# Seven more of the 21-matmul products in the two feed-forward parts of a decoder layer, and accumulating transfers among the down products

## The chip, the cores and the metric

The kernel runs on one core of a Trainium2 chip. The time is the device time of one execution in microseconds (us); the figure for a kernel is the median of several executions. The core has five engines with instruction streams of their own, each in a fixed order: TensorE (PE in the profile, its weight loads PEld), VectorE (DVE), ScalarE (ACT), GpSimd (POOL) and SyncE (SP). The streams meet only at semaphores. SP issues nearly all loads; POOL issues the accumulating transfers spoken of below.

## The reference

One decoder layer on 256 tokens of width 2048, all in float32: a feed-forward half, two token mixers side by side, a second feed-forward half, and a gated embedding, with a layer norm behind each. The part that is changed is the feed-forward half, which occurs twice (f1 and f2):

```
def swiglu(x, w_gu, w_down):
    g, u = jnp.split(x @ w_gu, 2, axis=-1)
    return (jax.nn.silu(g) * u) @ w_down

h = layer_norm(alpha * h + 0.5 * swiglu(h, w_ffn1_gu[i], w_ffn1_down[i]), ...)
... mixers ...
h = layer_norm(alpha * h + 0.5 * swiglu(h, w_ffn2_gu[i], w_ffn2_down[i]), ...)
```

`w_gu` is 2048 x 11264 and `w_down` 5632 x 2048. All weights (484 MB are read in one execution) pass through the core once.

## The kernel before

**Numbers.** Each float32 operand is split into a high and a low part of a shorter matmul type: ACT casts the high part (`hf_gu`, `hf_down`, line 124), DVE subtracts it from the original for the low part (`lf_gu`, `lf_down`, line 128). A product is three matmuls of 128 x 512: low by high, high by high, high by low (lines 418 to 420).

**Chunks and units.** Weights come in chunks of 128 x 1024 float32 (512 KB, one load on SP's queue). A unit of work takes two chunks: the same 256 rows of the sum for two groups of 512 columns. (In the names `lf2_gu_8_0_3` the parts are: f2, gate and up, block 8, chunk 0 of the unit, pair 3.) There are three kinds:

- P, a plain pair: 24 matmuls; two casts on ACT, two low parts on DVE.
- T, a plain pair whose second low part is made otherwise: ACT multiplies the chunk by -1 into the low part's tile (line 133), where it stands rounded, as minus the high part, and POOL's queue issues a transfer of 512 KB that adds the chunk itself to it (`transfer()`). It spares DVE a subtraction.
- S, a "seven": the four block products of a 2 x 2 split are formed by seven products, as in Strassen's and Winograd's scheme, so 21 matmuls. It needs sums of weight blocks, which DVE makes (lines 208 to 217): five operations on 128 x 512 and three on 128 x 1024, in the order u, u, v, `lf`, v, the low part of b, `luf`, `lvf`; ACT casts `hf`, `b`, `huf` and `hvf` for it. It also needs sums of blocks of the activations ("forms", lines 492 to 495, then a split), one group for two neighbouring pairs. The seven's own products collect in banks named `f28s`, `f1d0s` and so on, which are evicted at the end of a block (lines 526 to 530). The last seven of a block takes its low parts in an earlier order, so that 13 of its matmuls stand behind the last of them.

**Stages.** In each feed-forward half, gate and up are made in 11 blocks of 512 columns (j = 0 to 10), with 8 units each; then the down product in two halves of 1024 columns (d0 and d1, in the profile `f1d` and `f1e`), with 22 units each over the 5632 rows. Sevens stand in all gate and up blocks but the first, and in both down halves. Between units hang other pieces of work: in the down halves `before_unit(u)` converts the activations to high and low (`convert`, lines 99 and 100), makes the forms of groups 6 to 9, in f1 runs the rotary table in small pieces on DVE (lines 868 to 893), and at the start come the evictions of the last gate and up block (lines 526 to 530 and 1026 to 1028).

**What sets the order.** A list of all units in order (`plan`) is made beforehand. `fill()` issues loads ahead along this list as far as slots of the weight memory are free (`others(n)` sets how many), and `make_next()` makes a unit's parts some units ahead. So the order of the instructions on each engine is fixed when the program is built. `gu_units` gives the units of a gate and up block (sevens on pairs 0 to 3, order `PTSSPSST`), `down_units` those of the down halves.

Of the kernel before, what the change touches and what calls it, by code (L numbers as in the profile page):

```python
# [16 lines left out]
P = 128  # L17
S = 256
# [9 lines left out]
KF = FF // P  # L28
# [9 lines left out]
HELD_PAIRS = 2, 3  # L38
# [2 lines left out]

SEVEN = (0, 1, 2, 3)

AHEAD = {1: (4, 5), 2: (4,), 3: (4, 5), 4: (4,), 5: (4, 5), 7: (4, 5)}
AHEAD_SLOTS = 32

SEVEN_DOWN = (6, 7, 8, 9)

BIG = 3.0e38
MAGIC = 12582912.0  # L50
# [6 lines left out]
def layer(ctx: ExitStack, tc: tile.TileContext, io):  # L57
# [16 lines left out]
    def slot(shape, dt, name):  # L74
        return slots.tile(shape, dt, tag="slot", name=name)
# [22 lines left out]
    def split(dst_hi, dst_lo, src, lo_engine=None):  # L98
        act.copy(dst_hi, src)  # L99
        (lo_engine or dve).tensor_tensor(dst_lo, src, dst_hi, ALU.subtract)  # L100
# [243 lines left out]
    def slots_for_weights(n, ahead=45, far=90):  # L344
        room.update(slots=n, ahead=ahead, far=far)
# [139 lines left out]
    def seven_forms(full, hi, lo):  # L485


        a11, a21 = (full[:, 0::2, t * P : (t + 1) * P] for t in range(2))
        a12, a22 = (full[:, 1::2, t * P : (t + 1) * P] for t in range(2))
        raw = slot([P, 8, P], F32, "sums")  # L490
        f5, f6, f7, f3 = (raw[:, 2 * j : 2 * j + 2, :] for j in range(4))
        dve.tensor_tensor(f5, a21, a22, ALU.subtract)
        dve.tensor_tensor(f7, a11, a21, ALU.subtract)
        dve.tensor_tensor(f6, f5, a11, ALU.subtract)
        dve.tensor_tensor(f3, a12, f6, ALU.add)
        split(hi, lo, raw)
        return lambda e: [(hi[:, 2 * j + e, :], lo[:, 2 * j + e, :]) for j in range(4)]
# [401 lines left out]
    def gu_units(name, j):  # L899
        if j == 0:  # L900
            return [("P", p) for p in range(KD // 2)]
        if name == "f2" and j in AHEAD:
            return units_of(*(("PPSDSDSP", SEVEN[:3]) if j % 2 else ("PPSSDSSP", SEVEN)), AHEAD[j])
        return units_of("PTSSPSST", SEVEN)

    def gu_keys(name, j):
        return lambda n, p: (name + "_gu", j, n, p)

    def down_units(n_held):


        first = [("P", p) for p in range(2 * SEVEN_DOWN[0])]
        g = SEVEN_DOWN[0]
        sevens = [2 * h for h in SEVEN_DOWN[:3]] + [2 * SEVEN_DOWN[2] + 1, 2 * SEVEN_DOWN[3]]
        plain = [p for p in range(2 * g, KF // 2) if p not in sevens]
        plain = [p for p in plain if p < 2 * SEVEN_DOWN[2]] + sorted(
            (p for p in plain if p >= 2 * SEVEN_DOWN[2]), key=lambda p: p < 2 * SEVEN_DOWN[3] + 2
        )
        while sevens or plain:
            for kind, of in (("S", sevens), ("P", plain)):  # L920
                if of:
                    first.append((kind, of.pop(0)))
        plain = [p for p in range(KF // 2) if p // 2 not in SEVEN_DOWN]
        second = [("P", p) for p in plain[:2]]
        rest = plain[2:]
        for g in SEVEN_DOWN:
            for e in range(2):
                second += [("S", 2 * g + e), ("P", rest.pop(0))]
        return first, second + [("P", p) for p in rest[:-n_held]], rest[-n_held:]

    def down_keys(name, b):
        return lambda n, p: (name + "_down", 2 * b + n, p)

    def plan_ffn(name):
        for j in range(KF // 4):
            block_units(gu_units(name, j), gu_keys(name, j))
        first, second, held = down_units(HELD_PAIRS[name == "f2"])
        block_units(first, down_keys(name, 0))
        block_units(second, down_keys(name, 1))
        plan.extend(Single(down_keys(name, 1)(n, p)) for n in range(2) for p in held)  # L940

    def ffn(name, i, ht, norm, keep, residual, keepers, away):
# [3 lines left out]
        raws = []  # L946
        made = {}
# [27 lines left out]
        def convert(g):  # L975
            hi, lo = (slot([P, 4, S], F32R, f"{name}a{w}{g}") for w in "hl")
            split(hi, lo, raws[g])
            acts[g] = hi, lo

        for j in range(KF // 4):  # L980
# [20 lines left out]
            def before(u, j=j, offset=KD // 2 - len(units)):  # L1001
# [7 lines left out]
                if j == 0 and u == 7:  # L1009
# [12 lines left out]
            if got:  # L1022
                g, v = got
# [5 lines left out]
            else:  # L1029
                v = slot([P, 2, 512], F32, f"{name}v{j}")  # L1030
# [12 lines left out]
        y = {}  # L1043
        space = big.tile([P, 2 * len(SEVEN_DOWN), 8, P], F32R, tag="ht", name=name + "forms")
        made = {}
        first, second, held = down_units(HELD_PAIRS[name == "f2"])
# [12 lines left out]
        def before_unit(u):  # L1059
            if u == 0 and name == "f1":  # L1060
                lazy.append(rotary_table("r"))
            g = u // 2 + 2
            others(2 * KF // 4 - max(0, KF // 4 - 1 - g) + (2 if u >= 10 else 0))
            if u % 2 == 0:
                if 2 <= u < 2 + 2 * len(SEVEN_DOWN):
                    at = u // 2 - 1
                    made[SEVEN_DOWN[at]] = seven_forms(raws[SEVEN_DOWN[at]], space[:, 2 * at], space[:, 2 * at + 1])
                if g < KF // 4:
                    convert(g)
            if u in (11, 12):  # L1070
                y[u - 11] = load_columns(residual, u - 11, name + "y")

# [98 lines left out]
    def mixers(ht, norm, residual, keepers, away):  # L1171
# [691 lines left out]
```

## Time and profile before

| what | value |
|---|---|
| median of 3 runs | 2256.92 us (2256.03 to 2258.23) |
| the profiled execution | 2261.72 us |
| its span | 2259.6 us |
| granted clock of PE, mean | 0.998 |
| PE busy | 2243.5 us (99%) |
| DVE busy | 1995.2 us (88%) |
| ACT busy | 1345.4 us (60%) |
| accumulating transfers of gate and up | 28, 8.0 us each from issue to landing |
| f1's first down half (PE) | 459.70 to 577.30 us |
| f2's blocks 8 to 10 (second seven of block 8 to their end) | 1814.10 to 1926.15 us |
| f2's first down half | 1926.15 to 2042.43 us |

Times in the profile are of one execution, counted from the start of its span; a row gives start, duration, engine, line, operation, what it writes and reads, and in brackets the time that the engine stood before it and what released it. Rows of one line and kind that follow each other are drawn together (x2, x3). Windows give each engine's busy time in a stretch. A PE at 99% is a PE that is nearly always occupied, so what is worth knowing is in which stretches another engine is as full as it is.

### The profile page before, as it was taken

The numbers are of one execution on the slowest core, as the hardware profiler recorded it, in microseconds if no ns is written. First come the engines' busy times: TensorE is split into PE (matmuls) and PEld (weight loads), VectorE is DVE, ScalarE is ACT, GpSimd is POOL, SyncE is SP. The second block draws the span as 40 slices with busy tenths as digits, with TensorE's granted clock in tenths as the row PEclk, the third lists the DMA queues.
The fourth block names the chain that finished last, engine by engine and source line by source line (L and its number), as shares of the span: only waits on it lengthen the run. The fifth ranks groups of instructions, "written<-read, shape, count | busy, mean of one in ns | idle before, by whom it ended". The sixth has DMA issues, their size and how long they took to land.

```text
span 2259.6 us, 28888 instructions
## 1 busy us (share of the span) xinstructions
PE 2243.5 (99%) x10291; PEld 1856.3 (82%) x10291; DVE 1995.2 (88%) x2636; ACT 1345.4 (60%) x1586; POOL 26.7 (1%) x37
## 2 busy tenths in 40 slices
PE   9999999999999999999999999999999999999998
PEld 7888888888888788888788888788888887888887
DVE  6999999989988999889779788689998899889877
ACT  6776776766554554535556554466666677655543
POOL 0000000000000000000000000000000000000000
PEclk9999999999999999999999999999999999999999
DMA  9787887775676779866447568787979978656772
GB/s 312 227 259 240 231 262 225 217 248 188 214 290 255 260 254 312 277 231 207 138 143 247 172 221 288 268 288 248 304 260 272 309 227 245 221 187 219 290 265 73
DMA packets 260920, 541.92 MB, mean 240 GB/s; under 512 B 62620, under 2 KB 67100, under 8 KB 260776
## 3 DMA queue, kind: packets, MB, share of 16 engines
q1 hardware_dynamic: 254760, 522.82, 68.7%
q0 software_dynamic: 4032, 14.68, 3.5%
q10 hardware_dynamic: 1984, 2.58, 0.3%
q8 instruction: 81, 1.33, 0.2%
q14 instruction: 63, 0.52, 0.1%
HBM read 484.43 MB, written 29.36 MB: 227 GB/s over the span
## 4 chain that ended last, share of the span: by engine, by line
PE 89%; DVE 5%; DMA 3%; issue 1%; ACT 1%; SPq 0%; ACTq 0%; DVEq 0%
DMA rf_gu<-in_f_gu 3%; PE rqk L369 3%; PE f1g L420 2%; PE f1g L419 2%; PE f1g L418 2%; PE f1u L419 2%; PE f1u L418 2%; PE f1u L420 2%; PE f2g L419 2%; PE f2g L418 2%; PE f2g L420 2%; PE f2u L419 2%; PE f2u L418 2%; PE f2u L420 2%; PE aqk L369 2%; PE f2d L418 2%
## 5 line engine op out<-in xcount | busy, mean ns | idle before, releaser
L128 DVE TENSOR_TENSOR lf_gu<-rf_gu,hf_gu 128x1024 fp32r<-128x1024 f32 x236 | 281.6, 1218 | 16.0 <-ACT hf_gu L124 15.0
L124 ACT CAST hf_gu<-rf_gu 128x1024 fp32r<-128x1024 f32 x264 | 271.2, 1047 | 40.7 <-DMA rf_gu<-in_f_gu 37.5
L124 ACT CAST hf_down<-rf_down 128x1024 fp32r<-128x1024 f32 x150 | 153.1, 1050 | 66.8 <-DMA rf_down<-in_f_down 51.9
L128 DVE TENSOR_TENSOR lf_down<-rf_down,hf_down 128x1024 fp32r<-128x1024 f32 x150 | 178.0, 1219 | 14.2 <-ACT hf_down L124 6.5
L128 DVE TENSOR_TENSOR lw_in_f<-rw_in_f,hw_in_f 128x1024 fp32r<-128x1024 f32 x140 | 166.4, 1217 | 3.1 <-ACT hw_in_f L124 3.1
L124 ACT CAST hw_in_f<-rw_in_f 128x1024 fp32r<-128x1024 f32 x140 | 142.0, 1051 | 33.2 <-DMA rw_in_f<-in_w_in_f 24.9
L214 ACT CAST hvf_gu<-vf_gu 128x1024 fp32r<-128x1024 f32 x76 | 80.1, 1054 | 84.6 <-DVE vf_gu L213 73.3
L211 ACT CAST huf_gu<-uf_gu 128x1024 fp32r<-128x1024 f32 x76 | 80.1, 1054 | 55.3 <-DVE uf_gu L209 52.8
L216 DVE TENSOR_TENSOR luf_gu<-uf_gu,huf_gu 128x1024 fp32r<-128x1024 f32 x76 | 92.6, 1218 | 1.1 <-ACT huf_gu L211 0.8
L217 DVE TENSOR_TENSOR lvf_gu<-vf_gu,hvf_gu 128x1024 fp32r<-128x1024 f32 x76 | 92.6, 1218 | 0.0
L418 PE MATMUL f1g<-hf_gu,xt 128*128 128x512 f32 x232 | 90.5, 390 | 0.4 <-ACT hf_gu L99 0.4
L420 PE MATMUL f1g<-lf_gu,xt 128*128 128x512 f32 x232 | 90.5, 390 | 0.2 <-DVE lf_gu L128 0.2
L419 PE MATMUL f1g<-hf_gu,xt 128*128 128x512 f32 x232 | 90.3, 389 | 0.0
L418 PE MATMUL f2g<-hf_gu,ht 128*128 128x512 f32 x214 | 83.7, 391 | 0.0
L420 PE MATMUL f2g<-lf_gu,ht 128*128 128x512 f32 x214 | 83.5, 390 | 0.0
L419 PE MATMUL f2g<-hf_gu,ht 128*128 128x512 f32 x214 | 83.5, 390 | 0.0
L419 PE MATMUL f1u<-hf_gu,xt 128*128 128x512 f32 x192 | 74.7, 389 | 0.0
L420 PE MATMUL f1u<-lf_gu,xt 128*128 128x512 f32 x192 | 74.7, 389 | 0.0
L418 PE MATMUL f1u<-hf_gu,xt 128*128 128x512 f32 x192 | 74.7, 389 | 0.0
L418 PE MATMUL f2u<-hf_gu,ht 128*128 128x512 f32 x168 | 65.7, 391 | 0.0
L420 PE MATMUL f2u<-lf_gu,ht 128*128 128x512 f32 x168 | 65.4, 389 | 0.0
L419 PE MATMUL f2u<-hf_gu,ht 128*128 128x512 f32 x168 | 65.4, 389 | 0.0
(1562 smaller groups left out, 6707.0 us busy)
## 6 DMA issues: line engine op xcount, KB each, us to landing
rf_gu<-in_f_gu SPq DMA_DIRECT2D x360, 512.0 KB
rf_down<-in_f_down SPq DMA_DIRECT2D x176, 512.0 KB
rw_in_f<-in_w_in_f SPq DMA_DIRECT2D x148, 512.0 KB
rw_rv<-in_w_rv SPq DMA_DIRECT2D x32, 512.0 KB
rw_ret<-in_w_ret SPq DMA_DIRECT2D x32, 512.0 KB
rw_mix<-in_w_mix SPq DMA_DIRECT2D x32, 512.0 KB
rw_pg<-in_w_pg SPq DMA_DIRECT2D x32, 512.0 KB
lf_gu<-rf_gu POOLq DMA_DIRECT2D x28, 512.0 KB, 8.0
```

The costliest lines, as they stand in the source:

```text
L124: act.copy(self.hi, self.raw)
L128: dve.tensor_tensor(self.lo, self.raw, self.hi, ALU.subtract)
L211: act.copy(uh, u)
L214: act.copy(vh, v)
L216: dve.tensor_tensor(ul, u, uh, ALU.subtract)
L217: dve.tensor_tensor(vl, v, vh, ALU.subtract)
L369: pe.matmul(ps[f], hi[:, kk, f * P : (f + 1) * P], rhs(k), start=k == 0, stop=k == n_k - 1,)
L418: pe.matmul(o, al, bh, start=first, stop=False)
L419: pe.matmul(o, ah, bh, start=False, stop=False)
L420: pe.matmul(o, ah, bl, start=False, stop=self.left == 0)
```

## The change

The change gives sevens to units that were plain pairs, and transfers to others.

- **f1's first down half**: before, 12 plain pairs, then S and P in turn (sevens on pairs 12, 14, 16, 17, 18). Now P0 T1 P2 T3, then S12 T4 S13 P5 S14 T6 S15 P7 S16 T8 S17 P9 S18 T10, then P19 P11 P20 P21: seven sevens and six transfers.
- **f2's first down half**: before as in f1. Now P0 T1 P2 T3 S12 P4 S13 T5 S14 P6 S15 T7 S16 P8 S17 T9 S18 P10 S19 T11 P20 P21: eight sevens, six transfers.
- The groups of forms are made before units 2, 5, 9 and 13 (before: 2, 4, 6 and 8), and the conversions at the units of `CONVERT_AT`; the number of slots follows them.
- **f2's gate and up blocks 8 and 10**: five sevens instead of four, order P T S S S S S T instead of P T S S P S S T. The fifth is on pair 4, whose forms are there from other blocks.

In all there are 7 more sevens (21 fewer matmuls) and 12 more accumulating transfers. The second down halves keep their units.

```diff
+FIVE = {"f1": (), "f2": (8, 10)}
...
+FORMS_AT = 2, 5, 9, 13
+CONVERT_AT = {2: 6, 3: 2, 6: 7, 7: 3, 10: 8, 11: 4, 14: 9, 15: 5, 18: 10}
...
             return units_of(*(("PPSDSDSP", SEVEN[:3]) if j % 2 else ("PPSSDSSP", SEVEN)), AHEAD[j])
+        if j in FIVE[name]:
+            return units_of("PTSSSSST", SEVEN + (4,))
         return units_of("PTSSPSST", SEVEN)
...
-    def down_units(n_held):
-        first = [("P", p) for p in range(2 * SEVEN_DOWN[0])]
+    def down_units(name):
+        n_held = HELD_PAIRS[name == "f2"]
         g = SEVEN_DOWN[0]
-        sevens = [2 * h for h in SEVEN_DOWN[:3]] + [2 * SEVEN_DOWN[2] + 1, 2 * SEVEN_DOWN[3]]
-        plain = [p for p in range(2 * g, KF // 2) if p not in sevens]
...
-        while sevens or plain:
-            for kind, of in (("S", sevens), ("P", plain)):
-                if of:
-                    first.append((kind, of.pop(0)))
+        sevens = [2 * g + e for e in range(8)]
+        plain = [p for p in range(KF // 2) if p not in sevens]
+        if name == "f1":
+            plain.insert(11, sevens.pop())
+        first = [("PT"[p % 2], p) for p in plain[:4]]
+        rest = plain[4:]
+        while sevens:
+            first += [("S", sevens.pop(0)), ("TP"[len(sevens) % 2], rest.pop(0))]
+        first += [("P", p) for p in rest]
...
         def before_unit(u):
             if u == 0 and name == "f1":
                 lazy.append(rotary_table("r"))
-            g = u // 2 + 2
-            others(2 * KF // 4 - max(0, KF // 4 - 1 - g) + (2 if u >= 10 else 0))
-            if u % 2 == 0:
-                if 2 <= u < 2 + 2 * len(SEVEN_DOWN):
-                    at = u // 2 - 1
-                    made[SEVEN_DOWN[at]] = seven_forms(raws[SEVEN_DOWN[at]], space[:, 2 * at], space[:, 2 * at + 1])
-                if g < KF // 4:
-                    convert(g)
+            if u in FORMS_AT:
+                at = FORMS_AT.index(u)
+                made[SEVEN_DOWN[at]] = seven_forms(raws[SEVEN_DOWN[at]], space[:, 2 * at], space[:, 2 * at + 1])
+            others(KF // 4 + 2 + sum(v <= u for v in CONVERT_AT) + (2 if u >= 10 else 0))
+            if u in CONVERT_AT:
+                convert(CONVERT_AT[u])
```

The file grows by four lines ahead of the changed places, so a row with line 128 before has line 132 now, 133 has 137, 208 has 212 and 526 has 530.

How the order of instructions moves at three places. First, DVE in f2's block 8, from the end of the second seven on. Before, with the plain pair 6 there, of the third seven the first two rows:

```order
L217 TENSOR_TENSOR lvf_gu_0_1_16083<-vf_gu_0_1_16079,hvf_gu_0_1_16082 128x1024
L128 TENSOR_TENSOR lf_gu_0_6_16116<-rf_gu_0_6_16047,hf_gu_0_6_16076 128x1024
L128 TENSOR_TENSOR lf_gu_1_6_16150<-rf_gu_1_6_16061,hf_gu_1_6_16114 128x1024
L208 TENSOR_TENSOR uf_gu_0_2_16179<-rf_gu_1_2_16097 128x512
L209 TENSOR_TENSOR uf_gu_0_2_16179<-rf_gu_0_2_16095,rf_gu_1_2_16097 128x512
```

Now the third seven follows the second at once, then the fourth and the fifth; here the end of the fourth, the fifth (pair 4), and the last pair:

```order
L221 TENSOR_TENSOR lvf_gu_0_3_16192<-vf_gu_0_3_16188,hvf_gu_0_3_16191 128x1024
L212 TENSOR_TENSOR uf_gu_0_4_16233<-rf_gu_1_4_16227 128x512
L213 TENSOR_TENSOR uf_gu_0_4_16233<-rf_gu_0_4_16225,rf_gu_1_4_16227 128x512
L214 TENSOR_TENSOR vf_gu_0_4_16234<-rf_gu_0_4_16225,uf_gu_0_4_16233 128x512
L132 TENSOR_TENSOR lf_gu_0_4_16243<-rf_gu_0_4_16225,hf_gu_0_4_16229 128x1024
L217 TENSOR_TENSOR vf_gu_0_4_16234<-vf_gu_0_4_16234,rf_gu_0_4_16225 128x512
L219 TENSOR_TENSOR bf_gu_0_4_16231<-rf_gu_1_4_16227,bf_gu_0_4_16231 128x512
L220 TENSOR_TENSOR luf_gu_0_4_16236<-uf_gu_0_4_16233,huf_gu_0_4_16235 128x1024
L221 TENSOR_TENSOR lvf_gu_0_4_16238<-vf_gu_0_4_16234,hvf_gu_0_4_16237 128x1024
L132 TENSOR_TENSOR lf_gu_0_7_16280<-rf_gu_0_7_16250,hf_gu_0_7_16275 128x1024
```

Five sevens stand in a row there, where two low parts of a plain pair parted them. Second, ACT at the end of that block. Before, the multiplication of the last pair's second chunk (line 133):

```order
L211 CAST huf_gu_0_2_16181<-uf_gu_0_2_16179 128x1024
L214 CAST hvf_gu_0_2_16183<-vf_gu_0_2_16180 128x1024
L124 CAST hf_gu_0_7_16210<-rf_gu_0_7_16152 128x1024
L133 ACTIVATE lf_gu_1_7_16212<-rf_gu_1_7_16196 128x1024
L211 CAST huf_gu_0_3_16217<-uf_gu_0_3_16215 128x1024
L214 CAST hvf_gu_0_3_16219<-vf_gu_0_3_16216 128x1024
```

and now (line 137):

```order
L215 CAST huf_gu_0_3_16189<-uf_gu_0_3_16187 128x1024
L218 CAST hvf_gu_0_3_16191<-vf_gu_0_3_16188 128x1024
L128 CAST hf_gu_0_4_16229<-rf_gu_0_4_16225 128x1024
L203 CAST bf_gu_0_4_16231<-rf_gu_1_4_16227 128x512
L215 CAST huf_gu_0_4_16235<-uf_gu_0_4_16233 128x1024
L218 CAST hvf_gu_0_4_16237<-vf_gu_0_4_16234 128x1024
L128 CAST hf_gu_0_7_16275<-rf_gu_0_7_16250 128x1024
L137 ACTIVATE lf_gu_1_7_16277<-rf_gu_1_7_16252 128x1024
```

It stood ahead of the last seven's two late casts, and stands behind them now. Third, ACT at the start of f1's first down half (pair 1's chunks, and the copy `eve` with which the evictions begin). Before:

```order
L99 CAST f1ah_4007<-f1a_1258 128x1024
L124 CAST hf_down_0_4032<-rf_down_0_3974 128x1024
L124 CAST hf_down_1_4036<-rf_down_1_4003 128x1024
L526 COPY eve<-f110s_3728 128x512
L124 CAST hf_down_1_4063<-rf_down_1_4005 128x1024
```

and now:

```order
L103 CAST f1ah_4007<-f1a_1258 128x1024
L128 CAST hf_down_0_4032<-rf_down_0_3974 128x1024
L137 ACTIVATE lf_down_1_4034<-rf_down_1_4005 128x1024
L128 CAST hf_down_1_4039<-rf_down_1_4003 128x1024
L530 COPY eve<-f110s_3728 128x512
```

The chunk with number 4005 is the pair's second; its work on ACT stood behind the copy, and stands ahead of it now.

More of the change, by code (lines that the diff above doesn't have):

```diff
@@ L907, in gu_keys @@
         return lambda n, p: (name + "_gu", j, n, p)
-    def down_units(n_held):
-        first = [("P", p) for p in range(2 * SEVEN_DOWN[0])]
+    def down_units(name):
+        n_held = HELD_PAIRS[name == "f2"]
         g = SEVEN_DOWN[0]
-        sevens = [2 * h for h in SEVEN_DOWN[:3]] + [2 * SEVEN_DOWN[2] + 1, 2 * SEVEN_DOWN[3]]
-        plain = [p for p in range(2 * g, KF // 2) if p not in sevens]
-        plain = [p for p in plain if p < 2 * SEVEN_DOWN[2]] + sorted(
-            (p for p in plain if p >= 2 * SEVEN_DOWN[2]), key=lambda p: p < 2 * SEVEN_DOWN[3] + 2
-        )
-        while sevens or plain:
-            for kind, of in (("S", sevens), ("P", plain)):
-                if of:
-                    first.append((kind, of.pop(0)))
+        sevens = [2 * g + e for e in range(8)]
[7 more added lines that the diff above has]
+        first += [("P", p) for p in rest]
         plain = [p for p in range(KF // 2) if p // 2 not in SEVEN_DOWN]
@@ L936, in plan_ffn @@
             block_units(gu_units(name, j), gu_keys(name, j))
-        first, second, held = down_units(HELD_PAIRS[name == "f2"])
+        first, second, held = down_units(name)
         block_units(first, down_keys(name, 0))
@@ L1045, in ffn @@
         made = {}
-        first, second, held = down_units(HELD_PAIRS[name == "f2"])
+        first, second, held = down_units(name)
         n_of = {}
```

## Prediction

> **What bounds the kernel now.** I read the page first, then the busy time of the engines in the stretches that the change touches, then the waits of PE, then the order in time on PE, DVE and ACT at the places where the new units stand.
>
> ```profile
> PE 2243.5 (99%) x10291; PEld 1856.3 (82%) x10291; DVE 1995.2 (88%) x2636; ACT 1345.4 (60%) x1586; POOL 26.7 (1%) x37
> ```
>
> The matmuls fill the span, and DVE, at 88%, is the only other engine near it. A unit taken from PE is therefore a gain just as long as DVE, which gets more work by it, still delivers in time. The share over the whole span cannot tell that; the stretches can. Here are f1's first half (three rows) and f2's (two).
>
> ```profile
> 460.00:483.00 23.00, 22.09 (x99) 17.97 (x97) 20.70 (x32) 15.38 (x16) 0.00 (x0) 1.00 0.78 258
> 483.00:526.00 43.00, 43.00 (x189) 35.44 (x190) 38.77 (x52) 28.14 (x31) 0.00 (x0) 1.00 0.58 186
> 526.00:577.00 51.00, 51.00 (x227) 42.23 (x226) 48.52 (x54) 31.48 (x34) 0.00 (x0) 1.00 0.62 221
> 1926.00:1991.00 65.00, 65.00 (x289) 53.81 (x288) 53.35 (x62) 45.04 (x46) 0.00 (x0) 1.00 0.57 187
> 1991.00:2042.00 51.00, 51.00 (x227) 42.23 (x226) 45.67 (x52) 30.03 (x31) 0.00 (x0) 1.00 0.59 215
> ```
>
> The columns are PE, PEld, DVE, ACT and POOL busy, then the granted clock and the DMA share. In f1's first half DVE is busy 108.0 of 117 us and PE hardly waits: one wait of 0.9 us is listed for it.
>
> ```profile
> PE f1d L420 <- DVE lf_down L128: 0.9, 1, 0.9
> ```
>
> DVE has 9 us to spare over that half, and all hangs on when it has them. In f2's first half it has 17 us.
>
> **Prices of the units.** PE in f2's block 8, at the starts of the second seven, of the plain pair behind it and of the third seven:
>
> ```profile
> 1814.10 0.39 PE L418 MATMUL f28s<-hf_gu,ht 128*128 128x512 f32 x1
> ...
> 1818.86 0.39 PE L418 MATMUL f2g<-hf_gu,ht 128*128 128x512 f32 x1
> ...
> 1824.30 0.39 PE L418 MATMUL f28s<-hf_gu,ht 128*128 128x512 f32 x1
> ```
>
> A seven is 4.76 us (21 matmuls of 0.2267), a plain pair 5.44 (24). One more seven saves 0.68, and seven more save 4.76.
>
> DVE in the same block, at the end of the second seven, at the start of the fourth, and behind it:
>
> ```profile
> 1815.15 1.22 DVE L128 TENSOR_TENSOR lf_gu<-rf_gu,hf_gu 128x1024 fp32r<-128x1024 f32 x1
> ...
> 1824.98 0.69 DVE L208 TENSOR_TENSOR uf_gu<-rf_gu 128x512 f32<-128x512 f32 x1
> ...
> 1831.39 3.49 DVE L128 TENSOR_TENSOR lf_gu<-rf_gu,hf_gu 128x1024 fp32r<-128x1024 f32 x3
> ```
>
> The fourth seven took 1831.39 - 1824.98 = 6.41 us on DVE, 1.65 more than on PE. The x3 row gives one low part of 1024: with the pipelining (3.49 for three, 1.22 for one) each takes 1.135. A plain pair is thus 2.27 on DVE, a pair with an accumulating transfer 1.135. Sevens alone starve PE; pairs between them pay the debt, 3.17 each (4.31 with a transfer).
>
> **f1's first half.** By units: 17 plain and 5 sevens were 38.6 + 32.1 = 70.7 us of DVE; 9 plain, 6 with a transfer and 7 sevens are 20.4 + 6.8 + 44.9 = 72.1. The load is nearly the same for 1.36 us less of PE. What changes is the order: the last seven (pair 18) was the unit before the last pair; now five pairs stand behind it. All sevens, forms and the rotary table come due earlier, and the 30 us of PE behind the last seven need little of DVE.
>
> DVE works in a fixed order, so I add it up from its first eviction of the gate and up part to the end of the last seven. Before, this ran from 457.65 to 565.58:
>
> ```profile
> 457.65:565.58 107.93, 107.02 (x472) 88.12 (x471) 99.92 (x129) 70.02 (x73) 0.00 (x0) 1.00 0.63 211
> ```
>
> It held, by the program, 30 low parts, 5 sevens, 9 conversions of activations (L100, as long as a low part), 4 groups of forms, the rotary table and 9 evictions. Of 8.0 us without work 4 x 1.1 stand inside the forms (the row is below); 3.5 are other waits. Afterwards the same stretch holds 13 low parts, 7 sevens and 7 conversions, and the rest unchanged: 107.93 - 17 x 1.135 + 2 x 6.41 - 2 x 1.135 = 99.2 with those waits, 95.7 without. I take 96.4, near the lower end, as the loads come no later than now, and keep both ends.
>
> Its start moves too. DVE's first row of that stretch, and ACT there:
>
> ```profile
> 457.65 0.69 DVE L527 TENSOR_TENSOR evw<-eve,f110s 128x512 f32<-128x512 f32 x1 [2.60 <-ACT eve L526]
> ```
>
> ```profile
> 456.09 1.05 ACT L124 CAST hf_down<-rf_down 128x1024 fp32r<-128x1024 f32 x1 [3.62 <-DMA rf_down<-in_f_down]
> 457.04 0.58 ACT L526 COPY eve<-f110s 128x512 f32<-128x512 f32 x1
> 458.22 1.05 ACT L124 CAST hf_down<-rf_down 128x1024 fp32r<-128x1024 f32 x1 [0.60 <-DMA rf_down<-in_f_down]
> ```
>
> The two casts are the chunks of pair 1, which ACT took as they landed, with the copy that DVE waited for (2.60 us) between them. Now pair 1 has a transfer: the multiplication of its second chunk (landed at 458.2) stands first, then the first chunk's cast, then the copy. By the spacings of these rows: 458.22 + 0.95 + 0.95 = 460.1, plus 0.58, so DVE starts at about 460.75, 3.1 later. Queued behind it are all of DVE's evictions and the low parts. Should the chunk land earlier, the lower end is 457.65.
>
> So the last seven is complete at 460.75 + 96.4 = 557.15. PE, if nothing held it, would come to that seven's last part some 13 us earlier, so DVE decides; from there PE's own work sets the time. In block 8 DVE had the fourth seven complete at 1831.39, and PE started the next unit at:
>
> ```profile
> 1834.61 0.39 PE L418 MATMUL f2g<-hf_gu,ht 128*128 128x512 f32 x1
> ```
>
> 3.22 us: the 13 matmuls that are left when the last low part comes. Then come five pairs: 5 x 5.44 = 27.2. The second half starts at 557.15 + 3.22 + 27.2 = 587.6. Before, the halves start at:
>
> ```profile
> 459.70 0.39 PE L418 MATMUL f1d<-hf_down,f1al 128*128 128x512 f32 x1
> ...
> 577.30 0.39 PE L418 MATMUL f1e<-hf_down,f1al 128*128 128x512 f32 x1
> ```
>
> **+10.3 us** (bounds +6.5 and +13). Without any wait PE would be there at 459.70 + 7 x 4.76 + 15 x 5.44 = 574.6, so 13 us are new waits, in pieces of 0.7 to 3: at the first seven, behind each group of forms (a group holds DVE 3.8 us, of which 1.1 stand, by the rows), and at the seven on pair 18.
>
> ```profile
> 476.76 0.41 DVE L492 TENSOR_TENSOR sums<-f1a 128x256 f32<-128x256 f32 x1
> ...
> 479.43 1.23 DVE L100 TENSOR_TENSOR f1forms<-sums,f1forms 128x1024 fp32r<-128x1024 f32 x1 [1.12 <-ACT f1forms L99]
> ```
>
> The next half cannot give this back: it has no waits now that could go.
>
> **Blocks 8 and 10 of f2.** Without the pair in their middle DVE runs three sevens in a row from the end of the second: in block 8 1815.15 + 3 x 6.41 = 1834.4, and the last pair starts 3.2 later, at 1837.6 instead of 1834.61: +3.0, PE's saving included. That last pair has a transfer. Its multiplication stood ahead of the fourth seven's casts on ACT; now it stands behind the fifth's.
>
> ```profile
> 1828.69 1.05 ACT L214 CAST hvf_gu<-vf_gu 128x1024 fp32r<-128x1024 f32 x1 [1.26 <-DVE vf_gu L213]
> ```
>
> The page's row of the accumulating transfers, with the time from issue to landing at its end:
>
> ```profile
> lf_gu<-rf_gu POOLq DMA_DIRECT2D x28, 512.0 KB, 8.0
> ```
>
> The cast ran 3.71 behind its seven's start. The fifth seven starts at 1815.15 + 12.8 = 1828.0, its cast at 1831.7, a cast of the pair and the multiplication follow (0.95 each), and the transfer is issued at about 1834.5 and lands 8.0 later, at 1842.5. PE uses it 14 matmuls into the pair, at 1837.6 + 3.2 = 1840.8: a wait of 1.7. Block 8: **+4.7** (bounds +2.5, where transfer and casts are early, and +5.5).
>
> Block 10 waits already (1.4 for one low part) and then runs slowly, so less is new.
>
> ```profile
> 1899.66 2.36 DVE L128 TENSOR_TENSOR lf_gu<-rf_gu,hf_gu 128x1024 fp32r<-128x1024 f32 x2
> ```
>
> ```profile
> 1920.71 0.39 PE L418 MATMUL f2g<-hf_gu,ht 128*128 128x512 f32 x1
> ```
>
> 1899.66 + 19.2 + 3.2 = 1922.1, which is +1.4; the transfer by the same distances lands at 1912.5 + 6.6 + 8.0 = 1927.1 and is wanted at 1925.3: **+3.2** in all (bounds +1.4 and +4).
>
> **f2's first half.** DVE's first eviction and PE's first matmul there, before:
>
> ```profile
> 1920.56 0.68 DVE L527 TENSOR_TENSOR evw<-eve,f210s 128x512 f32<-128x512 f32 x1
> ```
>
> ```profile
> 1926.15 0.39 PE L418 MATMUL f2d<-hf_down,f2al 128*128 128x512 f32 x1
> ```
>
> DVE now leaves block 10's sevens at 1918.9 and has five conversions and low parts (1.135 each) ahead of the eviction: 1924.6, with some standing 1925.3. To the end of the last seven it has 8 x 6.41 + 15 low parts and 8 conversions x 1.135 + 4 x 3.8 of forms + 6.3 of evictions = 98.9, so 2024.2. PE, starting 3.2 late, wants that seven's last part after 7 sevens, 11 pairs and 8 of its own 21 matmuls: 1926.15 + 3.2 + 33.3 + 59.9 + 1.8 = 2024.3. It just fits: here there is no rotary table on DVE, and three pairs stand behind the last seven instead of five. So -3 x 0.68 = -2.0, and 0.3 for small waits: **-1.7** (bounds -2.0 and +1.5).
>
> **The sum.** 10.3 + 4.7 + 3.2 - 1.7 = +16.5. The profiled execution took 2261.72 (span 2259.6), 4.8 above the runs' median of 2256.92; I carry the difference over: span 2276, profiled execution 2278, **runs 2273**.
>
> **The clock.** Waits can cost more than themselves:
>
> ```profile
> 1913.00:1916.40 3.40, 1.85 (x8) 0.89 (x7) 3.40 (x5) 3.18 (x4) 0.00 (x0) 1.00 1.02 270
> 1916.40:1919.80 3.40, 3.40 (x10) 2.62 (x9) 3.38 (x4) 3.40 (x5) 0.00 (x0) 0.51 1.02 316
> 776.30:779.70 3.40, 1.98 (x8) 1.03 (x6) 3.40 (x5) 2.75 (x3) 0.00 (x0) 1.00 0.93 343
> 779.70:783.10 3.40, 3.31 (x14) 2.74 (x15) 3.40 (x5) 3.40 (x5) 0.00 (x0) 1.00 0.09 35
> ```
>
> After 3.4 us with 1.85 of PE work the clock fell to half for 3.4 us, which cost about 1.5; after 1.98 it did not fall. The Trainium skill, page "TensorE: Matmul & The Clock Gate", section "Part 1: The HAM clock gate (the "warmup" mystery)", has the half rate come only after at least one idle window of about 3.4 us; the first two rows disagree, since PE worked for half of the window ahead. By the page the sum would stay as it is; by the rows three or four of my waits (2 to 4 us long) are near the edge.
>
> **Rivals.** *Half clock* (slower still): at the seven on pair 13 or 14 of f1, in block 8 and in block 10 the clock falls, 3 to 4 times 1.5, +4.5 to +6: 2278. For it: the row at 1916.40; against: the one at 779.70, and that PE waits in pieces.
>
> *f1's half is nearly absorbed*: DVE runs through its list faster than I count, because the copy at its head is not late (3.1 us) and the 8.0 us in which it stood are all filled. f1 then gives 10.3 - 11.1 = -0.8, blocks 8 and 10 stall: -0.8 + 4.7 + 3.2 - 1.7 = +5.4, 2262.3. Against it: the forms wait for a cast of their own sums, which nothing in the list can fill, and beside them DVE stands only 3.5 us in 107.93.
>
> *The spare time of DVE pays for all* (the other side): PE asks for a seven's parts in the order in which DVE makes them, and if the casts run far enough ahead (ACT is at 60%), DVE starts each row of sevens with a lead instead of none. It decides from a lead of some 8 us on; then nothing waits, and the 4.76 saved and 1 of f1's present wait are the gain: 2251. Against it: three sevens lose 3 x 1.65 = 5.0 against PE, the fifth's last part is wanted 3 us before its end, and at 1815.15 DVE is only 3.7 us ahead of PE's end of the second seven (1818.86).
>
> **How the numbers follow.** Forecast 0.62, half clock 0.18, absorbed 0.12, other side 0.08. The forecast's own bounds add up to +8.4 and +24, which is 2265 to 2281. The half clock lies within them; the absorbed half is reached by going down to 2262. So the range is 2262 to 2281. A measurement of this kernel tells 0.2%, 4.5 us, from no change: slower means above 2261.4. That is the forecast, the half clock and half of the third case, 0.86; the other half of it, 0.06, is no change; faster has 0.08.
>
> **What would show it.** Right: DVE's first eviction near 460.7; PE waiting in most units of f1's first half on lf_down, luf_down and lvf_down, some 13 us of it; f1e starting near 587; in block 8 the last pair near 3 us later against the block's start, and a wait of 1 to 2 us there for a transferred low part; in f2's first half hardly a wait. Wrong: f1e at 577 or earlier; sevens on DVE shorter than 6.4; PE waiting for loads, which I count at nothing since they land some 4 to 6 us after issue and are issued a unit or more ahead; or DVE itself standing for tiles that PE has not released, which would lengthen every sum above.

## The result, and the profile after

The changed kernel takes 2285.62 us (median of 4 runs, 2283.33 to 2286.07) against 2257.52 for the kernel before in the same session: ratio 1.0123, 95% interval 1.0107 to 1.0138, which is 28 us slower. The forecast was slower by 16, with a range up to 2281; the sign was right, the size outside the range.

The page of the kernel after, its engines; the answer to the row that the prediction began with:

```profile
PE 2248.7 (98%) x10270; PEld 1853.8 (81%) x10270; DVE 2011.2 (88%) x2666; ACT 1365.6 (60%) x1612; POOL 37.0 (2%) x49
```

PE ran 21 matmuls fewer, was busy 5.2 us more (at half clock the same matmuls take longer, and the one ahead of a wait counts with its full 0.39 us instead of 0.2267), and the span grew by 23.9. The shares have hardly moved and tell nothing; the places do. The first matmuls of the stages that were touched, in the order in time on PE of the kernel after (f1's two down halves, f2's blocks 8, 9 and 10, f2's two down halves):

```profile
459.00 0.39 PE L422 MATMUL f1d<-hf_down,f1al 128*128 128x512 f32 x1
...
584.34 0.39 PE L422 MATMUL f1e<-hf_down,f1al 128*128 128x512 f32 x1
...
1814.14 0.39 PE L422 MATMUL f28s<-hf_gu,ht 128*128 128x512 f32 x1
...
1863.72 0.39 PE L422 MATMUL f29s<-hf_gu,ht 128*128 128x512 f32 x1
...
1904.52 0.39 PE L422 MATMUL f210s<-hf_gu,ht 128*128 128x512 f32 x1
...
1943.30 0.39 PE L422 MATMUL f2d<-hf_down,f2al 128*128 128x512 f32 x1
...
2065.43 0.39 PE L422 MATMUL f2e<-hf_down,f2al 128*128 128x512 f32 x1
```

The differences of such rows give the length of each stage. The table has them for the profiled execution of before, for a second profile of the same kernel (the first experiment below), and for after. A block counts from the first matmul of its first seven to that of the next block's, block 10 to the first of the down half.

| stage | before | before again | after | after less before again | forecast |
|---|---|---|---|---|---|
| f1, first down half | 117.60 | 116.28 | 125.34 | +9.1 | +10.3 |
| f2, block 8 | 41.59 | 42.05 | 49.58 | +7.5 | +4.7 |
| f2, block 9 | 40.80 | 40.80 | 40.80 | 0 | 0 |
| f2, block 10 | 34.42 | 31.84 | 38.78 | +6.9 | +3.2 |
| f2, first down half | 116.28 | 116.28 | 122.13 | +5.9 | -1.7 |
| span | 2259.6 | 2254.9 | 2283.5 | +28.6 | +16.5 |

The waits of PE in these stages after (us in total, times, longest): f1's down half, then block 8, then block 10, then f2's down half; waits below 0.3 us are left out.

```profile
PE f1d L424 <- DVE lf_down L132: 4.5, 5, 2.6
PE f1d0s L424 <- DVE luf_down L220: 1.1, 1, 1.1
PE f1d L422 <- DVE f1al L104: 0.5, 1, 0.5
```

```profile
PE f2u L424 <- DMA lf_gu<-rf_gu: 2.4, 1, 2.4
PE f28s L424 <- DVE lf_gu L132: 2.1, 2, 1.1
PE f28s L424 <- DVE luf_gu L220: 1.4, 1, 1.4
```

```profile
PE f210s L424 <- DVE lf_gu L132: 3.4, 4, 1.1
PE f210s L424 <- DVE luf_gu L220: 1.4, 1, 1.4
PE f2u L424 <- DMA lf_gu<-rf_gu: 0.4, 1, 0.4
```

```profile
PE f2d L424 <- DVE lf_down L132: 4.7, 4, 2.0
```

PE waits for DVE, as forecast, but for the transferred low part of the last pair (`f2u <- DMA lf_gu`), 2.4 us in block 8 and 0.4 in block 10. What was not forecast is the last row: f2's down half.

Between the waits the clock falls to half at four places (near 502, 1850, 1933 and 2028). Two of them, each with the 3.4 us ahead of it; columns as in the prediction's windows:

```profile
498.60:502.00 3.40, 1.52 (x7) 1.26 (x8) 3.23 (x4) 3.40 (x6) 0.00 (x0) 0.99 0.86 304
502.00:505.40 3.40, 3.40 (x10) 2.67 (x9) 3.40 (x5) 2.66 (x3) 0.87 (x1) 0.51 0.26 57
```

```profile
1846.90:1850.30 3.40, 1.48 (x6) 1.25 (x7) 3.40 (x5) 0.85 (x1) 0.00 (x0) 0.99 0.96 190
1850.30:1853.70 3.40, 3.40 (x9) 2.62 (x8) 2.25 (x5) 2.51 (x3) 0.00 (x0) 0.51 0.19 24
```

### The profile page after: what moved, and what is told of

Read it like the earlier page. It is cut to its first block, busy times and chain, and to the rows that moved or that the text cites. A ratio compares the mean times of both kernels' runs of the same rounds, so it can differ in the third digit from the quotient of the medians.

```text
span 2283.5 us, 28965 instructions
## 1 busy us (share of the span) xinstructions
PE 2248.7 (98%) x10270; PEld 1853.8 (81%) x10270; DVE 2011.2 (88%) x2666; ACT 1365.6 (60%) x1612; POOL 37.0 (2%) x49
## 4 chain that ended last, share of the span: by engine, by line
PE 86%; DVE 7%; DMA 4%; issue 3%; ACT 1%; ACTq 0%; DVEq 0%; POOL 0%; SPq 0%; POOLq 0%
PE f1g L422 3%; PE f1g L423 3%; PE f1g L424 3%; PE rqk L373 3%; PE f1u L423 2%; PE f1u L422 2%; PE f1u L424 2%; DMA rf_gu<-in_f_gu 2%; PE f2g L422 2%; PE f2g L424 2%; PE f2g L423 2%; PE f2u L424 2%; PE f2u L423 2%; PE f2u L422 2%; PE aqk L373 2%
## 5 line engine op out<-in xcount | busy, mean ns | idle before, releaser
L132 DVE TENSOR_TENSOR lf_down<-rf_down,hf_down 128x1024 fp32r<-128x1024 f32 x133 | 158.1, 1218 | 14.5 <-ACT hf_down L128 6.1
L373 PE MATMUL rqk<-ht,hw_in_f 128*128 128x512 f32 x256 | 64.3, 392 | 0.0
L422 PE MATMUL f2u<-hf_gu,ht 128*128 128x512 f32 x160 | 62.9, 393 | 0.0
```

Of the source, the lines that this page charges most:

```text
L132: dve.tensor_tensor(self.lo, self.raw, self.hi, ALU.subtract)
L373: pe.matmul(ps[f], hi[:, kk, f * P : (f + 1) * P], rhs(k), start=k == 0, stop=k == n_k - 1,)
L422: pe.matmul(o, al, bh, start=first, stop=False)
```

## The experiments

Theory A: each place loses what DVE's list there cannot deliver in time, whatever the other places do. Rivals: the twelve more accumulating transfers crowd the queues (B); blocks 8 and 10 leave DVE late, and the rest follows from that (C); later, the mere number of sevens.

**The kernel before once more**, with no edit, for a second profile.

> The kernel before once more (same instructions in the same order), for a second profile of it. If the first profile held waits of its own, then this one has its span nearer to the median less 2 us, about 2255, with blocks j=10 of f1 and f2 and the stretch between f1 and f2 shorter by 1 to 4 us in all. If the 4 us between profile and median belong to profiling, the span is near 2259 again.

Its span was 2254.9 and the execution 2257.0, which is the median. So nothing was added by profiling: the first profile held waits of its own, and the table shows where: 1.3 us in f1's down half, and 2.6 in block 10, where this time the clock stayed whole. The fair yardstick for a stage is the second profile: in the other profiles of this case in which they have their old units, f2's down half takes 116.28 each time and block 10 between 30.7 and 31.9, nine times, so the 34.42 of the first profile was the exception. Elsewhere the program is less steady: the stretch from f1's second down half to f2's block 8, the same in all, takes 1228.9 to 1232.6, so spans of single profiles cannot settle 1 to 3 us.

**The three parts apart.**

```diff
+NEW_DOWN = ()         # blocks 8 and 10 alone
+NEW_DOWN = ("f1",)    # f1's half alone, with FIVE = {"f1": (), "f2": ()}
+NEW_DOWN = ("f2",)    # f2's half alone, with the same FIVE
...
+        if name not in NEW_DOWN:
+            first = [("P", p) for p in range(2 * SEVEN_DOWN[0])]
+            for a, b in zip((12, 14, 16, 17, 18), (13, 15, 20, 21, 19)):
+                first += [("S", a), ("P", b)]
```

A half that is not new has its old conversions and forms too.

> Only blocks 8 and 10 of f2 have five sevens in a row; both down halves are as before. Theory A (each place loses what its own stretch lost in the trace, 8.0 and 4.4 us, and the places add up): +12 us against before, 10 to 14. Rival B (the twelve more accumulating transfers crowd the queues; none of them is here): +0 to +3. Rival C (blocks 8 and 10 leave DVE late for f2's down half, which loses 5.9 only for that): +12 plus 1 to 3 in f2's down half.

> Only f1's first down half is new; f2 is as before. Theory A: +7.7 us, 6 to 10, as in the trace of the whole change. Rival B: also about +7, half of what the two down halves lose; it then differs from A in the next run and in the one before. Rival C: +7.7.

> Only f2's first down half is new; f1 and the blocks 8 and 10 are as before. Theory A: +5.9 us, 4 to 7, as the waits there come from ACT's order inside the half (the cast of the first forms stands behind copies, three casts of activations stand behind the next unit's). Rival B: +6 to +7. Rival C: -2 to 0, since the half would start with DVE in time.

| only | median | before | difference | ratio, interval |
|---|---|---|---|---|
| blocks 8 and 10 | 2271.80 | 2256.95 | +14.9 | 1.0065 (1.0049 to 1.0082) |
| f1's half | 2263.99 | 2256.95 | +7.0 | 1.0037 (1.0024 to 1.0050) |
| f2's half | 2263.12 | 2256.95 | +6.2 | 1.0029 (1.0018 to 1.0039) |

The three sum to 28.1, as much as the whole loss; that they meet it to the tenth is luck, since each interval is 2.4 to 3.7 us wide to either side. B fails for the blocks, which have no more transfers than before and lose most; for the halves, with six more each, it fails only further below, where as many transfers in another order cost next to nothing. C fails, since f2's half loses 6.2 with nothing changed ahead of it. The blocks lose a little more than A's 10 to 14, whose 4.4 us for block 10 was taken from the first profile; by the second the changed kernel's blocks lose 7.5 + 6.9 = 14.4. The profile of the blocks alone does not repeat that split: there block 8 took 47.23 (+5.2), block 10 37.00 (+5.2), and 7.4 us were lost in the unchanged block 9 (more on it in the last section). That execution was 2.4 above the median; where the others lost their 15 us is not on record. f1's half alone took 127.36 in its profile (+11.1, in an execution 2.4 above the median), f2's 121.67 (+5.4).

**Blocks 8 and 10: how the sevens stand, and how many.** Two orders of the same kinds of units.

```diff
-            return units_of("PTSSSSST", SEVEN + (4,))
+            return units_of("PTSSTSSS", SEVEN + (4,))    # two and three
+            return units_of("PTSSSSPT", SEVEN)           # four, in a row
```

> Blocks 8 and 10 of f2 keep five sevens, but in the order P T S S T S S S, two and three in a row instead of five; both down halves as before. Theory A (VectorE pays 1.65 us for each seven in a row and each pair between pays it back): the third seven is complete 13.4 us after the block's first seven starts on TensorE, and wanted at 18.8; the fifth at 26.2, wanted at 26.3, so next to no wait: -2 to +1 us against before in all, where five in a row cost +15. Rival (five sevens are simply too much for VectorE in one block: 42.9 us of work against 40.1 on TensorE, in whatever order): +6 or more, 3 us and a half clock per block.

> Blocks 8 and 10 of f2 keep their four sevens, but in a row: P T S S S S P T; all else as before. Theory A (a row of sevens loses 1.65 us each on VectorE against TensorE): the fourth seven is complete 18.6 us after the first starts on TensorE and wanted at 16.1, a wait of 2.5 us in each block where 1.0 and 1.7 stand now: +2 to +3 us against before, up to +6 if the clock falls to half behind the wait. Rival (only the number of sevens in a block counts, not how they stand): no change, -1 to +1.

Five sevens as two and three: 2265.36 against 2257.53, ratio 1.0041 (1.0025 to 1.0057), +8 to +9. Four in a row: 2266.82 against 2256.58, ratio 1.0044 (1.0028 to 1.0060), +10. So the same four sevens cost 10 us more in a row than with a pair between them, and a fifth still costs 8 or 9 when the row is broken up. The waits with four in a row, block 8 first:

```profile
PE f210s L425 <- DVE lf_gu L133: 2.5, 3, 1.0
PE f210s L425 <- DVE luf_gu L221: 1.4, 1, 1.4
PE f28s L425 <- DVE luf_gu L221: 1.4, 1, 1.4
PE f28s L425 <- DVE lf_gu L133: 0.7, 1, 0.7
```

In block 8 the waits are 2.1 us where 2.5 was expected, and 0.7 in the second profile of before. Its stage grew by 3.1 (45.18 against 42.05): 1.4 of it are the waits that are new, most of the rest the half clock behind them (0.50 from 1824.53 to 1827.94). Block 10 grew by 5.4 (37.28 against 31.84), as the row began late there: DVE had the second seven complete 9.1 us after the block's first matmul, against 6.1 in block 8 and 7.0 in block 10 of the second profile, because a late chunk held up the evictions of block 9 ahead of it (the last section comes back to it). So PE is paced from the second seven on (three waits for `lf_gu`), the clock fell too, and some 2 us of this profile's loss belong to that chunk and not to the row. The expected +2 to +3 had the waits alone, +6 was the figure with half clock; both were too small.

With two and three the clock did not fall, but the debt moved on instead of vanishing: block 8 took 44.06, block 9, which has its old units, 43.82 (40.80 before), and f2's down half 118.53 (116.28). There PE waits for the late evictions of the last seven:

```profile
PE f2d L423 <- DVE evw L532: 1.8, 1, 1.8
PE f29s L425 <- DVE luf_gu L221: 1.4, 1, 1.4
PE f28s L425 <- DVE luf_gu L221: 1.4, 1, 1.4
```

The rival's sum, 42.9 us of DVE for 40.1 of PE, was the better guide to the size; its half clock did not come, and block 10 took 31.26, no longer than before. This order also puts a seven last in each block, so that its late evictions fall on the next stage. No run parts that from the number of sevens.

**f2's half: the forms.** Its units kept, the forms moved.

```diff
-FORMS_AT = 2, 5, 9, 13
+FORMS_AT = 2, 6, 10, 14      # with the conversion of their group
+FORMS_AT = 3, 6, 10, 14      # and the first one unit later
```

> Only f2's first down half is new, as in the run with that alone (+6.2 us), but the second to fourth groups of forms are made one unit later, before units 6, 10 and 14, directly ahead of the conversion of their group. Theory A (the half loses by the order on ScalarE and VectorE, not by its load): the three waits of 1.0 us for a cast of activations go, and the low parts that TensorE waits for (2.2 at most) come ahead of the forms' 3.8 us: 4 to 6 us less than with the half alone, 0 to +2 against before. Rival (eight sevens are too many there): no change, +5 to +6.

> As the kernel before this one, and the first group of forms is also one unit later, before unit 3, so that VectorE makes the first seven's parts while ScalarE is still busy with copies. Theory A: VectorE's wait of 3.3 us beyond the usual 1.1 at the first forms goes as well, -1 to -2 us against before. Rival, that this wait has no one waiting behind it: the same as the kernel before this one.

The first took 2259.18 against 2257.53, ratio 1.0007 (0.9997 to 1.0016): of the 6.2 us that the half loses alone, 4.5 are back, by nothing but the place of three groups of forms. The second took 2263.58 against 2257.53, ratio 1.0024 (1.0014 to 1.0033): moving the first group as well gives 4 us of it away again. In the profiles the half takes 118.48 and 120.74, against 121.67 with the half alone. PE then waits for the forms themselves, a consumer that the expectation had not looked for, and DVE's wait did not go: it stands 4.0 us for a cast of activations where it had stood for the cast of the forms.

```profile
PE f2d L423 <- DVE f2forms L105: 1.3, 1, 1.3
```

```profile
1936.93 1.23 DVE L105 TENSOR_TENSOR f2al<-f2a,f2ah 128x1024 fp32r<-128x1024 f32 x1 [4.03 <-ACT f2ah L104]
```

**f1's half: the same units, later.** Eight pairs first, then a seven and a pair in turn; as many sevens and transfers as in the change. The forms come before units 4, 8, 12 and 16, and the conversions move with them (left out here).

```diff
...
+pairs = [p for p in plain if p != 19] + [19]
+first = [("PT"[p in (1, 3, 5, 7, 8, 10)], p) for p in pairs[:8]]
+for p, s in zip(pairs[8:], range(12, 19)):
+    first += [("S", s), ("PT"[p in (1, 3, 5, 7, 8, 10)], p)]
...
```

> Only f1's first down half is new, with the same seven sevens and six accumulating transfers on as many pairs, but eight pairs come first and then a seven and a pair in turn, the last seven ahead of the last pair; conversions and forms follow that order. Theory A (what costs in f1 is the early place of the sevens, with 27 us of pairs behind the last): VectorE's list gets as long as before, its end comes about as late as TensorE wants it: -1.5 to +1 us against before, where the half alone cost +7.0. Rival (the load: sevens and transfers are the same in number): +5 to +7.

2255.77 against 2257.53, ratio 0.9989 (0.9980 to 0.9998). The loss of 7 us was the order: with as many sevens and transfers the kernel is about 2 us faster than before. It is the only version here whose interval lies below 1, by a hair. Its one profile, of an execution 2.5 us above the median, does not show the gain in the half itself: 119.24 us against 116.28, with one wait of 2.4 and half clock behind it.

**Can more be had?** The same with the forms earlier, f2's half in the late order too, and both.

```diff
+FORMS_AT = 2, 5, 8, 11       # f1, instead of 4, 8, 12, 16
+FORMS_AT = 3, 6, 9, 12       # f2: six pairs first, then S and a pair in turn
```

> f1's first down half as in the run with the late sevens, with the forms of the four groups made before units 2, 5, 8 and 11 instead of 4, 8, 12 and 16. The profile of that run shows one wait of 2.5 us, at the sixth seven, behind the last forms on VectorE, and half clock for 2.5 us behind it. Theory A (it is the order of VectorE's list): both go, the half takes 115 to 116 us in the trace (116.3 before, 119.2 there), -1.4 to -3 us against before. Rival (the load): the wait moves to another unit and stays as long, 0 to -1.5 us.

> Only f2's first down half is new, with its eight sevens and six accumulating transfers, but six pairs come first and then a seven and a pair in turn, forms before units 3, 6, 9 and 12. Theory A: with VectorE at 17 us to spare over the half (and 1 us less of load than before) nothing waits: the half takes 114.2 us in the trace (116.3 before, 121.7 in the changed kernel's order), -2 us against before. Rival (eight sevens are too many): waits of 2 us or more stay, 0 to +3.

> The two before this one together: all of the change but the five sevens in a row, in the late order. Theory A (the places add up): -3 to -5 us against before, about 2253. Rival: no better than before.

2257.72 (ratio 1.0004, 0.9994 to 1.0014), 2257.57 (0.9999, 0.9990 to 1.0009) and 2260.50 (1.0012, 1.0004 to 1.0021) against 2257.36. None is faster; theory A as I had sized it fails here, and the rival's words fit: the wait goes to another unit and stays as long. The profiles agree: f1's half takes 119.79 with the earlier forms (115 to 116 expected), f2's 117.20 in the late order (114.2 expected), each 116.28 in the second profile of before. In the kernel with f1's forms earlier and in the one with f2's late order, the longest wait that is left in each half:

```profile
PE f1d L425 <- DVE lf_down L133: 2.7, 1, 2.7
```

```profile
PE f2d0s L425 <- DVE lf_down L133: 1.8, 1, 1.8
```

Each stands behind a group of forms. DVE in the first of the two kernels, from the end of a seven to the low part that PE waits for:

```profile
526.36 0.42 DVE L497 TENSOR_TENSOR sums<-f1a 128x256 f32<-128x256 f32 x1
...
529.03 1.23 DVE L105 TENSOR_TENSOR f1forms<-sums,f1forms 128x1024 fp32r<-128x1024 f32 x1 [1.11 <-ACT f1forms L104]
530.17 1.22 DVE L133 TENSOR_TENSOR lf_down<-rf_down,hf_down 128x1024 fp32r<-128x1024 f32 x1
```

A seven of 6.4 us and forms of 3.8 stand ahead of that low part, and DVE's lead over PE was less than that. The two halves together came out about 3 us worse than either alone, hardly beyond the intervals; in that profile the two stages lost 1.2 and 1.6 us against before. Why is open.

## Why the prediction was right or wrong

**Right: what decides.** "DVE works in a fixed order, so I add it up." In f1's half DVE's last seven ended at 553.92 in the trace, and the second half began 30.4 us later, at 584.34; the prediction had 3.22 + 27.2 = 30.4. In block 8 the fifth seven ended at 1839.88 and the last pair began at 1843.10, again 3.22. In f2's half the last seven ended at 2045.71; with 3.22 and three pairs of 5.44 the next stage would begin at 2065.25, and it began at 2065.43. There PE did not wait for the last seven: its last wait ended at 2027.38, and the half clock behind it (2027.71 to 2031.12) brought PE to the seven's last part just after DVE. So in the halves the half clock cost 0.2 us at most: where DVE's list decides, PE's slow stretches are taken out of waits that it would have had anyway. In block 10 the sum does not hold: the fifth seven ended at 1932.71 and the last pair began at 1937.18, 4.47 later, because the clock was half from 1932.13 to 1935.55, on the very matmuls behind DVE's end.

**Right in sum, by errors that cancel, which is luck: f1's half.** Forecast +10.3, measured +9.1 in the profile and +7.0 alone, by the medians. The list was 1.7 us longer than the 96.4 that I took, and its start was not late. DVE's first eviction and its last seven's end, and ACT's multiplication that I expected at 458.2:

```profile
455.85 0.69 DVE L531 TENSOR_TENSOR evw<-eve,f110s 128x512 f32<-128x512 f32 x1 [0.77 <-ACT eve L530]
...
553.92 1.22 DVE L104 TENSOR_TENSOR f1al<-f1a,f1ah 128x1024 fp32r<-128x1024 f32 x1
```

```profile
453.34 1.06 ACT L137 ACTIVATE lf_down<-rf_down 128x1024 fp32r<-128x1024 f32 x1 [0.84 <-DMA rf_down<-in_f_down]
```

The step "the multiplication of its second chunk (landed at 458.2) stands first" took a landing of the old program for one of the new; the chunk landed 4.9 us earlier. The bounds had an early landing, with DVE's start at 457.65; it came 1.8 earlier still. PE's first matmul of the half came 0.7 earlier, which makes the stage longer, and the yardstick is 1.3 shorter than the first profile had it. The 13 us of new waits were not there either: the half took 10.4 more than its 114.9 us of matmuls, and the waits listed above, in seven places, are some 6 of it.

**Wrong: f2's half, the largest miss (-1.7 forecast, +5.9 measured).** The step that failed is "To the end of the last seven it has 8 x 6.41 + 15 low parts and 8 conversions x 1.135 + 4 x 3.8 of forms + 6.3 of evictions = 98.9". The list took 105.5:

```profile
1940.18:2045.71 105.53, 100.42 (x430) 80.84 (x429) 94.44 (x118) 72.05 (x77) 3.54 (x5) 0.98 0.73 218
```

DVE's first eviction came 0.9 us later against PE's start than forecast, and the list itself was 6.6 longer. These 6.6 are times in which DVE stood in the middle of its list for ACT, which I had left at the 1.1 that the forms always wait:

```profile
1956.97 1.23 DVE L104 TENSOR_TENSOR f2forms<-sums,f2forms 128x1024 fp32r<-128x1024 f32 x1 [4.46 <-ACT f2forms L103]
...
1981.52 1.23 DVE L104 TENSOR_TENSOR f2al<-f2a,f2ah 128x1024 fp32r<-128x1024 f32 x1 [1.00 <-ACT f2ah L103]
```

4.46 - 1.1 = 3.4 at the first forms, and 1.0 three times at a conversion of activations. The sums for the first forms are done at 1952.5. In ACT's order their cast stands behind two casts of the first seven (1.5 us from there on) and two copies for the transposition of the last block (1.9):

```profile
1952.53 0.61 ACT L203 CAST bf_down<-rf_down 128x512 fp32r<-128x512 f32 x1
1953.05 1.04 ACT L128 CAST hf_down<-rf_down 128x1024 fp32r<-128x1024 f32 x1
1953.99 1.99 ACT L963 COPY f2w<-evw 128x1024 uint16<-128x1024 uint16 x2
1955.89 1.05 ACT L103 CAST f2forms<-sums 128x1024 fp32r<-128x1024 f32 x1
```

The three casts of activations stand behind three casts of the next seven in the same way, the first at 1980.44. I had moved the forms on DVE and had not looked at what stands ahead of their casts on ACT. The run with the forms beside the conversions took back 4.5 of the 6.2 us: in its profile DVE's three waits of 1.0 are gone and the half is 3.2 shorter than with the half alone. The first wait is no proven loss; the run that was to remove it only moved it.

**Too small: blocks 8 and 10 (+7.9 forecast, +14.4 measured; +14.9 alone).** The mechanism was right, as the two other orders show; the terms were mis-sized. In block 8, against the first profile (+8.0): 3.0 for the row of sevens was 3.7, because DVE entered it 0.7 later; the wait of 1.7 for the transfer was 2.5, because its issue came 26.35 us after the block's first seven instead of 25.2; and 1.7 for the half clock (58 matmuls from 1848.82 to the end took 14.9 us instead of 13.15), which I had kept out of the forecast as a rival. Here it counts in full, since behind it PE, not DVE, sets the pace. The two rows:

```profile
1840.49 0.86 POOL L138 DMA_DIRECT2D lf_gu<-rf_gu  x1 [40.37 <-ACT lf_gu L137]
```

```profile
1848.82 0.50 PE L424 MATMUL f2u<-lf_gu,ht 128*128 128x512 f32 x1 [2.39 <-DMA lf_gu<-rf_gu]
```

In block 10 the step that failed is its base: "Block 10 waits already (1.4 for one low part) and then runs slowly, so less is new." The slow stretch belonged to that one execution. Against the second profile 6.9 are new, not 3.2. Of the 3.7 missed 2.6 are this base; the rest is what the stage itself took beyond the forecast: DVE entered the row 1.0 later, the half clock cost 1.3, and the wait for the transfer was about 0.5 instead of 1.8.

**Wrong: the carried difference.** "4.8 above the runs' median; I carry the difference over" cost about 4.7. The excess was not of profiling but of waits in that execution, 1.3 and 2.6 us of them inside the stretches that the terms start from (the same 1.3 and 2.6 as above, not further ones). The terms were differences to stages with these waits, and I added them to a median without them.

**The rivals.** Half clock came, at four places; at the two in the down halves it cost next to nothing, in the blocks 1.7 and 1.3. The absorbed half and the spare time of DVE did not come. The condition that I named for the last, a lead of some 8 us, was not there at block 8's row: DVE was through the second seven at 1820.63 and PE at 1823.66, a lead of 3.0.

## What to carry to other kernels

Two engines with fixed lists are compared by the end of the slower list, place by place, and a unit that moves work from one to the other pays only as far as the other has a lead where it stands; a share of 88% over the span says nothing on that, and neither does the room in a stage whose work comes in lumps of 6 and 4 us. When a step moves on one engine, walk through the queue of every engine that feeds it: 6.6 of the 7.6 us missed in one stage were waits for casts that had come to stand behind other work of ACT. And before a profiled execution is made the base of a sum, a second one tells which of its waits belong to the kernel.

## What the runs showed of the hardware that was not expected

The clock falls after less than an idle window of PE. The windows above show 1.5 of 3.4 us with matmuls in them, six or seven, and then half clock. In the first profile of before 1.85 us in eight matmuls was followed by half clock. Where the window lies does not explain it alone. The four falls in the profile of the kernel after (501.95, 1850.21, 1932.13, 2027.71) are 395, 24 and 28 steps of 3.413 us apart, so they lie on a fixed grid. On that grid the windows ahead of them hold 1.39 to 1.47 us, and the one ahead of the fall in the first profile 1.86; but in the kernel after a window with 1.58 and one with 1.91 were followed by full clock:

```profile
1836.56:1839.97 3.41, 1.91 (x6) 0.95 (x6) 3.41 (x5) 2.79 (x3) 0.00 (x0) 1.00 0.97 226
1839.97:1843.39 3.42, 3.37 (x15) 2.79 (x16) 2.75 (x3) 3.42 (x5) 0.86 (x1) 1.00 1.04 365
2000.40:2003.81 3.41, 1.58 (x7) 0.96 (x6) 2.29 (x3) 3.33 (x4) 0.00 (x0) 1.00 0.89 275
2003.81:2007.23 3.42, 3.25 (x14) 2.72 (x15) 2.42 (x4) 2.03 (x3) 0.00 (x0) 1.00 0.81 297
```

So between 1.6 and 1.9 us of work both occur, and what decides there is open. The Trainium skill, page "TensorE: Matmul & The Clock Gate", section "Part 1: The HAM clock gate (the "warmup" mystery)", asks for at least one idle window of about 3.4 us; in these runs half of a window with waits in it was enough.

In the run with the five sevens alone, the profiled execution (2274.17, the longest of that kernel's) lost 7.4 us in block 9, which is unchanged. A chunk came late, ACT stood for it, and all behind it with it:

```profile
ACT lf_gu L138 <- DMA rf_gu<-in_f_gu: 11.3, 1, 11.3
```

SP's transposing transfer and POOL's accumulating one had been issued 0.1 us apart there (1868.40 and 1868.49), and the second took 14.9 us from issue to landing. With four sevens in a row the two were 0.25 apart at the same place, the second took 11.5, and ACT stood 7.3 us for the chunk:

```profile
1878.81 1.06 ACT L138 ACTIVATE lf_gu<-rf_gu 128x1024 fp32r<-128x1024 f32 x1 [7.25 <-DMA rf_gu<-in_f_gu]
```

In the second profile of before they were 0.7 apart, the second took 7.2 and ACT stood 4.5; in six other profiles, with 0.64 to 0.71 between them, it took 7.2 to 7.4. That the two collide when issued so close fits, but it is a guess: in the changed kernel two such transfers 0.16 apart, near 478, took no more than 7.8 for the second.
